# The first shift and scale of a two-layer backbone: from three engines to TensorE, inside the first projection's loop

## The chip, the core and the metric

One core of a Trainium2 chip runs the whole program in one launch. The metric is the device time of one execution in microseconds (us). The kernel before took 1386.01 us, the median of 3 runs (1384.87 to 1386.74).

## The reference, cut to what matters

Two layers work on 256 latent tokens `x` and 256 context tokens `ctx`, each 1024 wide. Each layer starts with a normalisation whose result is scaled and shifted by vectors that come from a conditioning vector; the first projection follows.

```python
silu_c = jax.nn.silu(c)
silu_cc = jax.nn.silu(c_ctx)
...
mx = (silu_c @ w_ada[l] + b_ada[l]).reshape(b, N_MOD, 1, D_MODEL)
mc = (silu_cc @ w_ada[l] + b_ada[l]).reshape(N_MOD, 1, 1, D_MODEL)
hx_n = _modulate(_rms_norm(h, norm1_g[l]), mx[:, 0], mx[:, 1])
hc_n = _modulate(_rms_norm(hc, norm1_g[l]), mc[0], mc[1])
...
ux = _split_cols(hx @ w_in)
uc = _split_cols(hc @ w_in)
```

`_modulate(h, shift, scale)` is `h * (1 + scale) + shift`. Shift and scale of layer 0 are two products of a vector of 1024 with a matrix of 1024 x 1024, for each of the two vectors `c` and `c_ctx`: the first two of the six parts of `w_ada[0]`. Behind the two layers stands a last normalisation.

## The kernel before, in words

Activations lie with the 1024 channels in eight blocks of 128 partitions and the 512 tokens (256 of the context, 256 latent) in the free dimension. The normalised and modulated input is kept as a pair `hn[k]` of a high part `hh` and a low part `hl`, in a reduced fp32 format, and so are the weights: a chunk of 128 x 1024 is loaded to `raw` (L99), ScalarE (ACT) casts it to the high part of `hl` (L117), VectorE (DVE) makes the low part (L107). A product is then three matmuls: high by high, high by low, low by high (`mm3`, L189 to L191). The program is recorded in the order in which it is written, engine by engine; there is no scheduler.

`start()` (from L417) does the head of layer 0. It loads `h`, sums the squares over the channels (L470 to L476), sums over the partitions with four matmuls (L269), takes the root with Newton steps on DVE (L257 to L259) and spreads the result `R` over the partitions (L283). silu of `c_ctx` and `c` is spread to all partitions as `cb[0]` and `cb[1]`.

Shift and scale of block k need the rows of two tiles of 128 x 1024 (`wa`, the transposed `w_ada`) multiplied with `cb` and summed. For `c` DVE does both in one instruction (L441); for `c_ctx` GpSimd (POOL) multiplies (L452) and ACT sums (L459). Two operations of 128x2 on DVE make the coefficients of it, `Ag` (L520) and `mods` (L522). `mod(k)` multiplies `h[k]` with `R` (L512, DVE), scales and shifts (L514, ACT, `v`), casts to `hh` (L516, ACT); L542 makes the low part on DVE.

The loop over the eight input blocks k then multiplies block k with eight weight blocks and adds to eight output banks at once, which are all of PSUM: `outs` is four `pg`, two `ps`, one `pt`, one `po`. In turn k the queues hold the coefficients of k+1 behind the work of k, so the small operations of DVE stand behind L441's long ones and wait for ACT's sums, and these for POOL's products.

```python
for i in range(8):
    mm3(outs[i], blk(k, i), hn[k], k == 0, k == KT - 1)
```

Behind the loop `mixer` takes the banks away: the first four go to `nakd` (ACT, L625) and `nakl` (DVE, L628), the others to `naq` (L635, L638). POOL clears `nakl` and `up` (L612, L614) and copies `nakd` (L629). `tokmajor` (L225) needs the four `pg` banks at once for the next 96 matmuls, with the weight chunks 8 to 11. The tiles of `start()` lie in a pool of their own (`sp`) which the mixer's tiles (`nakl`, `naq`, `up`) reuse.

Of the kernel before, what the change touches and what calls it, by code (L numbers as in the profile page):

```python
# [8 lines left out]
F32 = mybir.dt.float32  # L9
# [9 lines left out]
KT = 8  # L19
# [13 lines left out]
def hybrid_dit_kernel(ctx: ExitStack, tc: tile.TileContext, hT, wst, adaf, crow_d, vec_d,  # L33
# [69 lines left out]

    def prep_lo(i=total):
        while late and late[0][0] <= i:
            _, r, t = late.pop(0)
            V.tensor_tensor(t[:, 1], r, t[:, 0].bitcast(F32), op=ALU.subtract)  # L107

    def prep_to(i, wait=False):
        if not wait:  # L110
            prep_lo(i)
        while st["prep"] <= min(i, total - 1):
# [4 lines left out]
            S.copy(t[:, 0], r)  # L117
# [299 lines left out]
    def start():  # L417
        with tc.tile_pool(name="st", bufs=1) as sp:
            crow = sp.tile([1, 2048], F32, name="crow")
            nc.sync.dma_start(out=crow, in_=crow_d)  # L420
# [4 lines left out]
            make_identity(nc, ident)  # L425
            S.activation(tiny(1, "dummy"), eps, AF.Silu)

            acc = new_acc()
            gb = sp.tile([128, 8], F32, name="gb")
            V.scalar_tensor_tensor(gb, vec[:, V_BA + 8:V_BA + 16], 1.0, vec[:, V_N1:V_N1 + 8],  # L430
                                   op0=ALU.add, op1=ALU.mult)
            wa = {}
# [6 lines left out]
            def ada_v(k, ms=(0, 1)):  # L439
                for m in ms:  # L440
                    V.tensor_tensor_reduce(out=tmp().bitcast(BF16), in0=wa[k, m], in1=cb[1], scale=1.0,  # L441
                                           scalar=0.0, op0=ALU.mult, op1=ALU.add,
                                           accum_out=mods[0][:, m * 8 + k, 1:2])

            pr = {}

            def ada_p(k, ms=(1, 0)):
                if k >= KT:
                    return
                for m in ms:  # L450
                    t = pr[k, m] = sp.tile([128, 1024], F32, name="pr", tag="pr", bufs=4)
                    P.tensor_tensor(t, wa[k, m], cb[0], op=ALU.mult)  # L452

            def ada_s(k, ms=(1, 0)):
                if k >= KT:
                    return
                for m in ms:
                    t = pr[k, m]
                    S.activation(t, t, AF.Copy, accum_out=mods[0][:, m * 8 + k, 0:1])  # L459
# [889 lines left out]
```

## Time and profile before

| what | value |
|---|---|
| median of 3 runs | 1386.01 us (1384.87 to 1386.74) |
| the profiled execution: its time, its span | 1382.58 us, 1380.8 us |
| TensorE (PE) busy | 1322.7 us, 96% of the span |
| weight loads of PE (PEld) busy | 1147.2 us |
| DVE busy | 894.2 us |
| ACT busy | 597.2 us |
| POOL busy | 200.2 us |
| mean granted clock of PE | 0.987 |

Every trace time below counts from the start of the span of that one profiled execution, whose own time is 1.8 us longer than its span and 3.4 us below the median of the runs. A busy share is a mean over the whole span; what a stretch waits for is read from that stretch. In the rows, a line of the timeline gives the start, the length in which instructions of one kind follow each other, the engine, the source line, the operation, what it writes and reads, its shape and the count; at its end may stand the engine's idle time before it and what ended that.

### The profile page before, as it was taken

The page shows a single profiled execution, that of the slowest core. Times are in us where ns is not written, and L with a number is a line of the kernel's source. Part 1 is how long each engine was busy: PE and PEld are TensorE (multiplying, and loading weights), DVE is VectorE, ACT ScalarE, POOL GpSimd, SP SyncE. Part 2 cuts the span into 40 slices and gives each one's busy share as a digit, 9 for nine tenths or more (in the row PEclk, how much of TensorE's full clock was granted, in tenths as well). Part 3 has the DMA queues.
Part 4 walks back from the last instruction along what each step waited for, and adds up shares of the span by engine and source line. Part 5 has one row for each costly group of instructions (what it writes and reads, how often), then busy time and mean ns, then how long its engine had stood idle before and what let it go on. Part 6 is the DMA issues. An engine that isn't in the chain of part 4 may idle for free.

```text
span 1380.8 us, 19738 instructions
## 1 busy us (share of the span) xinstructions
PE 1322.7 (96%) x7658; PEld 1147.2 (83%) x7658; DVE 894.2 (65%) x1467; ACT 597.2 (43%) x929; POOL 200.2 (14%) x230
## 2 busy tenths in 40 slices
PE   4799999899999999999999999999999989999997
PEld 2578777688888888888888888988889989899997
DVE  8997554766877766565555653665538877655555
ACT  5484554544232435232123232465556545544453
POOL 6652302412000001000000000142134200000000
PEclk9999999999999999999999999999999999999999
DMA  7433322433545624355445653243435665455553
GB/s 261 168 110 117 98 71 83 128 123 122 183 162 162 201 71 138 124 171 165 155 139 172 211 183 99 70 140 108 142 122 185 217 237 177 151 184 195 183 171 106
DMA packets 62304, 207.27 MB, mean 150 GB/s; under 512 B 7041, under 2 KB 11521, under 8 KB 62209
## 3 DMA queue, kind: packets, MB, share of 16 engines
q1 hardware_dynamic: 50546, 163.97, 36.3%
q10 hardware_dynamic: 11664, 42.04, 9.2%
q8 instruction: 60, 0.98, 0.3%
q14 instruction: 34, 0.28, 0.1%
HBM read 204.94 MB, written 1.05 MB: 149 GB/s over the span
## 4 chain that ended last, share of the span: by engine, by line
PE 87%; DVE 8%; ACT 2%; issue 2%; DMA 0%; POOL 0%; SPq 0%; DVEq 0%; ACTq 0%; POOLq 0%
PE pg L189 26%; PE pg L190 26%; PE pg L191 26%; PE po L941 1%; DVE hl L107 1%; DVE tmp L441 1%; PE pt L675 1%; PE po L687 1%; DVE mods L522 1%; PE ps L643 1%; PE ps L644 1%; DVE rkl L876 0%; ACT hl L117 0%; DVE acc L476 0%; ACT hh L310 0%
## 5 line engine op out<-in xcount | busy, mean ns | idle before, releaser
L189 PE MATMUL pg<-hh,hl 128*128 128x256 f32 (+1 forms) x1568 | 530.9, 339 | 15.2 <-ACT hh L516 12.7
L191 PE MATMUL pg<-hl,hl 128*128 128x256 f32 (+1 forms) x1568 | 527.4, 336 | 2.2 <-DVE hl L542 1.6
L190 PE MATMUL pg<-hh,hl 128*128 128x256 f32 (+1 forms) x1568 | 526.2, 336 | 1.4 <-DVE hl L107 1.4
L107 DVE TENSOR_TENSOR hl<-raw,hl 128x1024 fp32r<-128x1024 f32 x276 | 342.3, 1244 | 174.8 <-ACT hl L117 169.8
L117 ACT CAST hl<-raw 128x1024 fp32r<-128x1024 f32 x276 | 287.6, 1046 | 207.5 <-PE pg L191 108.0
L189 PEld LDWEIGHTS pg<-hh,hl 128*128 128x128 f32 x1568 | 302.0, 193 | 48.7 <-ACT hh L516 15.1
L191 PEld LDWEIGHTS pg<-hl,hl 128*128 128x128 f32 x1568 | 301.7, 192 | 34.6 <-DVE hl L542 4.3
L190 PEld LDWEIGHTS pg<-hh,hl 128*128 128x128 f32 x1568 | 301.9, 193 | 32.1 <-DVE hl L107 2.1
L378 DVE CUSTOM_DVE_ANT_0 tmp<-ada,cb 128x1024 bf16<-128x1024 f32 x128 | 156.1, 1226 | 27.1 <-DMA ada<-in_adaf 17.8
L189 PE MATMUL pg<-fh,hl 128*128 128x256 f32 (+1 forms) x374 | 121.6, 325 | 0.0
L190 PE MATMUL pg<-fh,hl 128*128 128x256 f32 (+1 forms) x374 | 121.4, 325 | 0.0
L191 PE MATMUL pg<-fl,hl 128*128 128x256 f32 (+1 forms) x374 | 121.4, 325 | 0.0
L319 POOL TENSOR_TENSOR hl<-tmp,hh 128x256 fp32r<-128x256 f32 x20 | 14.8, 738 | 627.4 <-ACT hh L308 371.1
L291 ACT CAST fh<-sg 128x512 fp32r<-128x512 f32 (+1 forms) x44 | 22.6, 513 | 140.9 <-DVE sg L1150 140.9
L190 PEld LDWEIGHTS pg<-fh,hl 128*128 128x128 f32 x374 | 70.1, 188 | 7.2
L189 PEld LDWEIGHTS pg<-fh,hl 128*128 128x128 f32 x374 | 70.1, 187 | 7.1
L191 PEld LDWEIGHTS pg<-fl,hl 128*128 128x128 f32 x374 | 70.1, 187 | 7.1
L335 DVE SCALAR_TENSOR_TENSOR h<-pg,mods,h 128x256 f32<-128x256 f32 x72 | 32.7, 480 | 65.8 <-PE pg L191 65.7
L1150 DVE TENSOR_TENSOR sg<-pg,sg 128x512 f32<-128x512 f32 (+1 forms) x44 | 24.5, 557 | 51.1 <-PE pg L191 47.7
L1000 ACT ACTIVATE tmp<-pg 128x512 f32<-128x512 f32 (+1 forms) x48 | 23.5, 490 | 77.2 <-PE pg L191 76.2
L1147 ACT ACTIVATE sg<-pg 128x512 f32<-128x512 f32 (+1 forms) x44 | 21.6, 491 | 69.2 <-PE pg L191 69.2
L189 PE MATMUL pg<-hl,hh 128*128 128x512 f32 x128 | 50.6, 395 | 0.0
(241 smaller groups left out, 1643.4 us busy)
## 6 DMA issues: line engine op xcount, KB each, us to landing
raw<-in_wst SPq DMA_DIRECT2D x276, 512.0 KB, 3.6
ada<-in_adaf ACTq DMA_DIRECT2D x80, 512.0 KB, 3.8
wa<-in_adaf SPq DMA_DIRECT2D x16, 512.0 KB, 4.5
h<-in_hT SPq DMA_DIRECT2D x16, 256.0 KB, 5.0
bm<-in_bias SPq DMA_DIRECT2D x32, 128.0 KB, 2.0
out<-yt SPq DMA_DIRECT2D x4, 256.0 KB, 2.8
cs<-in_rope SPq DMA_DIRECT2D x2, 256.0 KB, 3.0
pw<-in_pw SPq DMA_DIRECT2D x2, 256.0 KB, 3.6
```

The lines of the kernel that those rows point to most:

```text
L107: V.tensor_tensor(t[:, 1], r, t[:, 0].bitcast(F32), op=ALU.subtract)
L117: S.copy(t[:, 0], r)
L189: TE.matmul(o, wh, xh, start=a, stop=False)
L190: TE.matmul(o, wl, xh, start=False, stop=False)
L191: TE.matmul(o, wh, xl, start=False, stop=z)
L291: S.copy(d0, src)
L319: P.tensor_tensor(hn[k][1][:, c], t[:, c], hi, op=ALU.subtract)
L335: V.scalar_tensor_tensor(h[k][:, c], o, mods[l][:, col + k, s:s + 1], h[k][:, c], op0=ALU.mult, op1=ALU.add)
L378: V.tensor_tensor_reduce(out=tmp().bitcast(BF16), in0=tiles[n], in1=cb[s], scale=1.0, scalar=0.0, op0=ALU.mult, op1=ALU.add, accum_out=mod ...
L1000: S.activation(sg[f][:, cl], o, AF.Sigmoid)
L1147: S.activation(e["s"][:, c], o, AF.Silu)
L1150: V.tensor_tensor(e["s"][:, c], o, e["s"][:, c], op=ALU.mult)
```

## The change

All of the first shift and scale is multiplied on PE. The weights come untransposed (`adan`, 1 MB per block k, one load instead of two of 512 KB). `csil` holds silu of the two vectors in two of 32 columns, the rest is zero. For block k, `nat_first` (new L459) multiplies eight pieces `csil[:, kb]` (128 x 32) with `wn[k][:, kb]` (128 x 256) in plain fp32; the pieces write four strips of 32 partitions of one bank, in turn, so each strip holds a part of the sum. `nat_copy` (L463) brings the bank to SBUF, and `nat_second` (L469) multiplies it with `sel`, which adds the four strips and turns the result by 90 degrees: two matmuls of two columns. The two small operations of DVE follow (L470, L472).

The bank that this needs is `outs[7]`. The loop therefore accumulates only seven output blocks; the weights of the eighth are kept (`w7`, high and low part) and its 24 matmuls follow behind the loop. The first eight weight chunks are cast in two pieces, 896 and 128 columns. `cb` is still needed later, and is now spread by 16 matmuls with the identity and copied by ACT. Two of the squares move from POOL to DVE.

```diff
+    def parts(j, t):
+        if j >= KT:
+            return [(t, slice(0, 1024))]
+        return [(t[:, :, :896], slice(0, 896)), (st["w7"][:, :, j], slice(896, 1024))]
...
-            S.copy(t[:, 0], r)
+            for a, b in parts(j, t):
+                S.copy(a[:, 0], r[:, b])
...
-            def ada_load(k):
-                for m in (1, 0):
-                    t = wa[k, m] = sp.tile([128, 1024], F32, name="wa", tag="wa", bufs=6)
-                    nc.sync.dma_start(out=t, in_=adaf[0, m * 8 + k])
...
+            def nat_load(k):
+                if k < KT:
+                    wn[k] = sp.tile([128, 8, 256], F32, name="wn", tag="wn", bufs=3)
+                    nc.sync.dma_start(out=wn[k], in_=adan[k])
...
+            outs = [pg() for _ in range(4)] + [pS(), pS(), pT(), pO()]
+            nat = outs[7]
+
+            def nat_first(k):
+                for kb in range(8):
+                    g = slice(32 * (kb % 4), 32 * (kb % 4) + 32)
+                    TE.matmul(nat[g, :256], csil[:, kb], wn[k][:, kb], start=(kb < 4), stop=(kb >= 4))
...
+            def nat_second(k, t):
+                o = nat[:, 256:260]
+                for i in range(2):
+                    TE.matmul(o[:, 2 * i:2 * i + 2], t[:, i * 128:(i + 1) * 128], sel, start=True, stop=True)
+                V.tensor_scalar(Ag[0][:, 0, k, :], o[:, 0:2], vcol(0, V_N1, k), gb[:, k:k + 1],
+                                op0=ALU.mult, op1=ALU.add)
+                V.tensor_scalar(mods[0][:, k, :], o[:, 2:4], vcol(0, V_BA, k), None, op0=ALU.add)
...
+            for k in range(KT):
+                nat_load(k + 3)
+                load_to(k + 3)
+                more = k + 1 < KT
+                if more:
+                    nat_first(k + 1)
                     prep_to(k + 1, True)
-                ada_p(k + 2)
-                if k + 1 < KT:
-                    ada_v(k + 1, (1,))
...
+                    t = mult(k + 1)
+                    tn = nat_copy()
+                block(k, 0)
+                block(k, 1)
+                if more:
+                    nat_second(k + 1, tn)
                     prep_lo()
...
-                for i in range(8):
-                    mm3(outs[i], blk(k, i), hn[k], k == 0, k == KT - 1)
+                    mod(k + 1, t)
+                for i in range(2, 7):
+                    block(k, i)
+            for k in range(KT):
+                mm3(outs[7], (w7[:, 0, k], w7[:, 1, k]), hn[k], k == 0, k == KT - 1)
```

On PE, at the end of turn 0 and the start of turn 1, there stood before the blocks of `pt` and `po` and at once the next input block (`hh1`):

```order
L191 MATMUL pt_233<-hl0_86,hl_224 128x512
L189 MATMUL po_234<-hh0_85,hl_224 128x512
L190 MATMUL po_234<-hh0_85,hl_224 128x512
L191 MATMUL po_234<-hl0_86,hl_224 128x512
L189 MATMUL pg_227<-hh1_87,hl_251 128x512
L190 MATMUL pg_227<-hh1_87,hl_251 128x512
L191 MATMUL pg_227<-hl1_88,hl_251 128x512
```

The same place now (`mm3` has become L196 to L198):

```order
L198 MATMUL pt_157<-hl0_86,hl_235 128x512
L459 MATMUL po_158<-wn_147,csil_129 32x256 x8
L196 MATMUL pg_151<-hh1_87,hl_265 128x512
L197 MATMUL pg_151<-hh1_87,hl_265 128x512
L198 MATMUL pg_151<-hl1_88,hl_265 128x512
L196 MATMUL pg_152<-hh1_87,hl_265 128x512
L197 MATMUL pg_152<-hh1_87,hl_265 128x512
L198 MATMUL pg_152<-hl1_88,hl_265 128x512
L469 MATMUL po_158<-sel_135,wt_321 128x2 x2
L196 MATMUL pg_153<-hh1_87,hl_265 128x512
```

The eighth block is gone from the turn; the product group of the block after next stands in its place, and two small matmuls stand behind the first two blocks.

On DVE one turn held before, with two long operations of L441, each followed by the reading of its sum, among the others:

```order
L520 TENSOR_SCALAR Ag_81<-mods_79,vec,gb 128x2
L522 TENSOR_SCALAR mods_79<-mods_79,vec 128x2
L512 TENSOR_TENSOR tmp<-h_113,Rs 128x512
L441 ISA tmp,mods_79<-wa,cb_78 128x1024
L441 ISA mods_79 128x1
L107 TENSOR_TENSOR hl<-raw,hl 128x1024
L542 TENSOR_TENSOR hl_94<-v,hh_93 128x512
L441 ISA tmp,mods_79<-wa,cb_78 128x1024
```

One turn of DVE now:

```order
L510 TENSOR_TENSOR tmp<-h_111,Rs 128x512
L463 COPY wt<-po 128x256
L470 TENSOR_SCALAR Ag_81<-po,vec,gb 128x2
L472 TENSOR_SCALAR mods_79<-po,vec 128x2
L113 TENSOR_TENSOR hl<-raw,hl 128x896
L113 TENSOR_TENSOR w_138<-raw,w_138 128x128
L519 TENSOR_TENSOR hl_94<-v,hh_93 128x512
```

The multiply with `Rs` now stands ahead of the coefficients, the long operations of L441 are gone, and a copy and a second piece of the weights' low part have come.

On DVE behind the loop, where the first banks are taken away, the waits (named in brackets, by the engine or DMA queue whose count is waited for) were:

```order
L394 TENSOR_TENSOR lga<-lga,vec 128x8 [waits DVE_49]
L628 TENSOR_TENSOR nakl_656<-pg,nakd_664 64x512 [waits PE_49,Activation_49,Pool_49]
L628 TENSOR_TENSOR nakl_657<-pg,nakd_665 64x512
L628 TENSOR_TENSOR nakl_658<-pg,nakd_666 64x512 [waits PE_49,Activation_49]
L628 TENSOR_TENSOR nakl_659<-pg,nakd_667 64x512
```

and are now:

```order
L401 TENSOR_TENSOR lga<-lga,vec 128x8 [waits DVE_49]
L628 TENSOR_TENSOR nakl_685<-pg,nakd_693 64x512 [waits DMAHW3_49,DMAHW5_49,PE_49,DMAHW7_49,Activation_49,Pool_49]
L628 TENSOR_TENSOR nakl_686<-pg,nakd_694 64x512
L628 TENSOR_TENSOR nakl_687<-pg,nakd_695 64x512 [waits Activation_49]
L628 TENSOR_TENSOR nakl_688<-pg,nakd_696 64x512
```

The order of the operations is the same. The count of PE that the first of them waits for was that of the last matmul of the first bank; in the built program it is now that of the last of the 24 matmuls behind the loop, since `nakl` lies where `w7` lay. POOL's first clearing operation (L610) waits for the same count.

## Rows read from the trace of the kernel before

**Rows 1.** The page: engine's busy time (share) xinstructions; a costliest group, busy, mean ns.

```profile
PE 1322.7 (96%) x7658; PEld 1147.2 (83%) x7658; DVE 894.2 (65%) x1467; ACT 597.2 (43%) x929; POOL 200.2 (14%) x230
...
L107 DVE TENSOR_TENSOR hl<-raw,hl 128x1024 fp32r<-128x1024 f32 x276 | 342.3, 1244 | 174.8 <-ACT hl L117 169.8
```

**Rows 2.** Windows: stretch, length, busy PE, PEld, DVE, ACT, POOL; PEclk, DMA share, GB/s.

```profile
10.00:20.00 10.00, 1.95 (x9) 1.78 (x8) 9.65 (x9) 5.87 (x10) 8.71 (x3) 1.00 1.02 413
30.00:79.00 49.00, 37.86 (x122) 27.11 (x122) 49.00 (x50) 26.81 (x46) 27.96 (x10) 0.90 0.45 150
79.00:95.00 16.00, 15.96 (x70) 13.25 (x71) 13.50 (x25) 14.29 (x24) 5.94 (x13) 1.00 0.51 171
```

**Rows 3.** Waits from 30 to 79 us: total us, times, longest.

```profile
PE pg L189 <- ACT hh L516: 12.7, 6, 3.8
```

**Rows 4.** Timeline: POOL's products, DVE's small operations beside and without them.

```profile
11.29 16.75 POOL L452 TENSOR_TENSOR pr<-wa,cb 128x1024 f32<-128x1024 f32 x6 [1.59 <-ACT sq L470]
...
20.14 2.26 DVE L258 SCALAR_TENSOR_TENSOR nt<-nt,ms 128x4 f32<-128x4 f32 x1
...
42.13 5.63 POOL L452 TENSOR_TENSOR pr<-wa,cb 128x1024 f32<-128x1024 f32 x2 [3.58 <-ACT pr L459]
...
43.11 2.34 DVE L520 TENSOR_SCALAR Ag<-mods,vec,gb 128x2 f32<-128x2 f32 x1
...
85.00 0.28 DVE L520 TENSOR_SCALAR Ag<-mods,vec,gb 128x2 f32<-128x2 f32 x1
...
86.11 1.10 ACT L514 ACTIVATE v<-tmp,mods,Ag 128x256 f32<-128x256 f32 x2 [0.17 <-DVE tmp L512]
...
87.89 0.69 DVE L542 TENSOR_TENSOR hl<-v,hh 128x512 fp32r<-128x512 f32 x1 [0.69 <-ACT hh L516]
```

**Rows 5.** Timeline of PE: the first blocks, the last two turns, the first matmul behind.

```profile
30.68 0.79 PE L189 MATMUL pg<-hh,hl 128*128 128x512 f32 x1 [3.78 <-ACT hh L516]
...
36.15 0.45 PE L189 MATMUL ps<-hh,hl 128*128 128x512 f32 x1
...
84.16 0.39 PE L189 MATMUL pg<-hh,hl 128*128 128x512 f32 x1
...
95.04 0.39 PE L189 MATMUL pg<-hl,hh 128*128 128x512 f32 x1
```

**Rows 6.** Timeline of the start (DVE, PE), and of a later normalisation at the full clock.

```profile
8.79 5.79 DVE L476 TENSOR_TENSOR acc<-acc,sq 128x512 f32<-128x512 f32 x4 [0.31 <-ACT sq L470]
...
14.64 1.87 PE L269 MATMUL ps<-ones,acc 128*128 128x1 f32 x8 [4.56 <-DVE acc L476]
24.85 2.05 PE L283 MATMUL pt<-ident,rstd 128*128 128x128 f32 x8 [8.34 <-DVE rstd L259]
...
506.94 0.50 PE L269 MATMUL ps<-ones,acc 128*128 128x1 f32 x4
...
508.82 0.60 PE L283 MATMUL pt<-ident,rstd 128*128 128x128 f32 x4
```

**Rows 7.** Timeline of PE: fp32 matmuls on strips of 64, neighbours, and 512 columns.

```profile
2.92 7.16 PE L481 MATMUL pg<-crow,ones 1*128 1x512 f32 x8 [2.92 <-DMA crow<-in_crow]
...
146.34 0.39 PE L191 MATMUL pg<-hl,hl 128*128 128x512 f32 x1
146.65 1.95 PE L687 MATMUL po<-pt,nav 128*64 128x256 f32 x16
148.53 0.66 PE L675 MATMUL pt<-ident,p 128*128 128x128 f32 x4
```

**Rows 8.** Timeline behind the loop: POOL and DVE.

```profile
89.34 4.44 POOL L612 MEMSET nakl<- 64x512 f32 x8
...
92.63 5.66 DVE L628 TENSOR_TENSOR nakl<-pg,nakd 64x512 fp32r<-64x512 f32 x8 [1.42 <-ACT nakd L625]
...
95.83 6.21 POOL L629 CAST nakd<-nakd 64x512 fp32r<-64x512 f32 x8
...
110.02 3.49 DVE L107 TENSOR_TENSOR hl<-raw,hl 128x1024 fp32r<-128x1024 f32 x3
```

More of the change, by code (lines that the diff above doesn't have):

```diff
@@ L116, in prep_to @@
             r = raw_t.pop(j)
-            S.copy(t[:, 0], r)
+            for a, b in parts(j, t):
+                S.copy(a[:, 0], r[:, b])
             late.append((j, r, t))
@@ L425, in start @@
             make_identity(nc, ident)
+            csil = sp.tile([128, 8, 32], F32, name="csil")
+            P.memset(csil, 0.0)
             S.activation(tiny(1, "dummy"), eps, AF.Silu)
@@ L439, in ada_v @@
[L439 to L452, printed above, removed]
@@ new lines, in start, with nat_copy @@
+            for k in range(3):
+                nat_load(k)
+                load_to(k)
+            outs = [pg() for _ in range(4)] + [pS(), pS(), pT(), pO()]
[4 more added lines that the diff above has]
+                    TE.matmul(nat[g, :256], csil[:, kb], wn[k][:, kb], start=(kb < 4), stop=(kb >= 4))
+            def nat_copy():
+                t = sp.tile([128, 256], F32, name="wt", tag="wt", bufs=2)
+                V.tensor_copy(t, nat[:, :256])
+                return t
@@ L468, in sq_k, with spread @@
+            sqrt_table()
+            for i in range(4):
+                for b in range(4):
+                    kb = 4 * (i % 2) + b
+                    TE.matmul(outs[i][:, b * 128:(b + 1) * 128], csil[:, kb, i // 2:i // 2 + 1].to_broadcast([128, 128]),
+                              ident, start=True, stop=True)
+            def spread(i):
+                S.copy(cb[i // 2][:, (i % 2) * 512:(i % 2) * 512 + 512], outs[i])
+            for k in range(KT):
                 t = sp.tile([128, 512], F32, name="sq", tag="sq", bufs=4)
-                if eng is S:
+                if k in (2, 5):
+                    V.tensor_tensor(t, h[k], h[k], op=ALU.mult)
+                else:
@@ L470, in sq_k @@
                     S.activation(t, h[k], AF.Square)
-                else:
-                    eng.tensor_tensor(t, h[k], h[k], op=ALU.mult)
                 if k == 0:
@@ L476, in sq_k, with mult, mod @@
                     V.tensor_tensor(acc, acc, t, op=ALU.add)
[L478 removed]
+                if k in (3, 4, 6):
+                    spread(max(k - 3, 0) - (k > 4))
+            o = outs[4]
             for i in range(4):
[L480 to L502 removed]
+                TE.matmul(o[:, i:i + 1], acc[:, i * 128:(i + 1) * 128], ones[:, 0:1], start=True, stop=True)
             y = norm_rstd(o, 4)
[L504 to L506 removed]
+            spread(3)
+            R = norm_bcast(y, range(4), outs[6])
+            nat_first(0)
+            t0 = nat_copy()
             prep_to(0, True)
             Rs = sp.tile([128, 512], F32, name="Rs")
[L510 to L511 removed]
+            def mult(k):
+                t = tmp()
                 V.tensor_tensor(t, h[k], R if k == 0 else Rs, op=ALU.mult)
+                return t
+            def mod(k, t):
+                v = sp.tile([128, 512], F32, name="v", tag="sq", bufs=4)
                 for s, c in enumerate((CTX, X)):
```

87 lines of the change are left out of this document (19 added, 68 removed).

## The prediction

> **What bounds the kernel now.** The page is read first. TensorE (PE) is busy 96% of the span [rows 1], so in most of the program nothing else shortens the time. The question is where PE isn't full, and the 10 to 95 us stretches of the windows view answer it [rows 2]: from 10 to 20 us PE works 1.95 of 10 us, from 30 to 79 us 37.86 of 49 us while VectorE (DVE) works all 49, and from 79 us on PE is full (15.96 of 16). The granted clock of 0.90 in the middle row says that part of the time ran at the lower level, 1.2 GHz. The waits of that stretch name the cause: PE stood 12.7 us for the shifted and scaled block `hh` of L516 [rows 3], and the two 128x2 coefficients before it come late on DVE. The timeline shows why DVE is late [rows 4]. In one turn L520, an operation of two columns, takes 2.34 us beside a POOL product (L452, 42.13 to 47.76 us); the same operation takes 0.28 us at 85.00, when POOL has stopped. At the start it is the same: L258, four columns, takes 2.26 us beside POOL's 16.75 us of products. So the head of the kernel, up to about 79 us, is bound by DVE, and largely by DVE being held while POOL multiplies. The reader should see that PE could do the 64 blocks in 64 x 0.68 = 43.5 us (below), and needs from 30.68 to 95.04.
>
> All sums below are for one number: when PE begins the work after the eight output blocks, 95.04 us now [rows 5]. From there PE is full, so I carry a shift of that moment to the end of the program unchanged.
>
> **The price of the old matmuls.** From 84.16 to 95.04 there are 48 starts, 0.227 us apart [rows 5]; a block of three costs 0.68, a turn of seven blocks 4.76, the last 24 matmuls 5.44. The first twelve at the low clock, with the wait for the first low part, took 30.68 to 36.15, 5.47 instead of 2.72: 2.75 us more.
>
> **The change, part by part.**
>
> *POOL's products, DVE's reduces and ScalarE's (ACT's) sums go.* These are what held the coefficients. All small DVE operations then cost what they cost at 85 us. A turn of DVE has left one multiply and one low part (0.69 each [rows 4]), a copy of 256 columns (at most 0.69), two small operations (0.28 each) and the low part of the weights (1.24 [rows 1], now in two pieces, perhaps 0.1 more): about 4.0 us, below PE's turn, so DVE stops being the bound. ACT has a weight cast, 1.10 for `v` and a cast, some 3 us; splitting its cast is hidden there.
>
> *The start.* The last four additions of the squares begin at 8.79 and take 5.79 us beside POOL [rows 6]; at the 0.7 of a 512-column operation they end at 11.6 instead of 14.58. The two squares that move from POOL to DVE fit its waits for `h` before that. Then, all at the low clock as before: four column sums 1.87, the root and three Newton steps 1.38 (from the end of L269 at 507.44 to L283 at 508.82, free of POOL), the broadcast 2.05 [rows 6]: 16.9. The first product group, 2.0 (below): 18.9; a copy and two small matmuls (half of 1.87) with their handovers: 20.4; two coefficients 0.5: 20.9; `v` to `hh`, 86.11 to 87.9 [rows 4]: **22.7** for the first block instead of 30.68. The 16 matmuls that spread silu(c) lie before 11.6: 32 records like L283's eight in 2.05 are 8.2 us, from about 3.5. The new 1 MB loads carry the bytes of the two halves they replace; at 413 GB/s [rows 2] the 3.1 MB of the first two pairs of loads need 8 us after `h`, which ends them before they are used.
>
> *The product groups.* Eight fp32 matmuls per turn, 256 columns, each on 32 of PE's 128 columns, four strips in turn. No such operation is in the trace; the nearest is L687: 16 records (two for each of eight fp32 matmuls), same 256 columns, strips of 64 in pairs. The matmul before it starts at 146.34, the one after the group at 148.53 [rows 7]: less 0.23 for the former, 1.96 us. Records in a row would take 16 x 0.227 = 3.6, since an fp32 record passes its columns twice: L481's eight records of 512 columns take 7.16 us, 0.9 each, where the first twelve of [rows 5] are 0.46 apart. So pairs run side by side: 8 rounds of 0.215 and 0.24 of entry and exit. If four strips run side by side as two do, 4 x 0.215 + 0.24 = **1.1 us**. Bounds: 0.9 without entry and exit, 3.9 with no overlap at all. I take 1.1, the pattern of the nearest row extended to four. At the low clock that is 2.0.
>
> The Trainium skill's "TensorE: Matmul & The Clock Gate", section "Measured speedup vs the span model", speaks against a full factor of four: four row strips gave 3.07 times, three column strips 2.38. By it the group would be an estimated 3.6 / 3.07 + 0.24 = 1.4 us, and the total about 3 us later; no run here shows four strips.
>
> *The second matmuls.* Two per turn, two columns each, four records: L269 at the full clock has four in 0.50 [rows 6]. Their input copy lies beside blocks 0 and 1 (1.36 us), so I charge no wait.
>
> *The chain inside a turn.* After the second matmuls the next block's chain runs beside blocks 2 to 6 and the next product group, 3.4 + 1.1 = 4.5 us. It costs 85.00 to 87.9 without the multiply, which now comes earlier, some 2.5 to 3.1 us for `hh`; the low part is wanted 0.45 later than `hh`. Slack is over 1 us, so I charge 0.1 a turn. The prepared weights come before the low part on DVE and fit the same slack.
>
> *The eighth block.* It moves 24 matmuls to the end; nothing is added to PE. But the kept weights lie in memory that the mixer's `nakl` tiles reuse: in the new program L628's first eviction waits for the very last of these matmuls, where it began at 92.63, before PE was through [rows 8]. The first bank is free after two of its eight operations (5.66 / 8 each): 0.2 + 1.42 = 1.6 us in which PE has no bank for `tokmajor`. Queued behind them on DVE are the evictions of `naq`, the decay logarithms and the low part of chunk 11 (first of three at 110.02 [rows 8], done 18.5 us after L628 began). PE wants it 16.8 us after `tokmajor` begins. So the true price is 0.2 + 18.5 - 16.8 = **1.95 us**. ACT's casts of `nakd`, on the contrary, get 7 us of cover. POOL's clearing of `nakl` and what follows it up to its copies (89.34 to 95.83), and the copies (6.21) [rows 8], had begun beside the last blocks; now they begin after them and end some 13 us later. The first scores that read them stand behind most of `tokmajor`'s 96 matmuls of 0.227, 21.8 us, so I charge nothing; with that cover gone it would be rival 4.
>
> **Sum.** 22.7 + 2.75 (low clock, first low part) + 56 x 0.68 = 38.1 + 6 x 1.1 (the first two groups lie in the start) = 6.6 + 7 x 0.5 = 3.5 + 0.7 + 5.44 = 79.8; with the eviction 1.95: **81.75 instead of 95.04, 13.3 us less**. The profiled execution, 1382.58 us, would become 1369.3. It lies 3.4 below the median of the runs shown, 1386.01; against that the time is **1372.7 us**.
>
> **Rivals.**
> 1. *The four strips run only two at a time*: 1.96 a group. Six groups add 5.2; the two of the start, at the low clock, 2.7. 7.9 in all, a gain of 5.4: 1380.6. For it: each fp32 matmul is two records that use the same strip, and two side by side is all the trace shows. Against: the pairs of L687 begin 0.215 apart, as long as one record, so it's the columns that limit and not the issue.
> 2. *The strips don't overlap*: 3.9 a group at full clock, 6.9 at the low one. Six add 16.8, the first two 4.9 and 4.3 (part of the latter lies beside the start's chain), so 26 against 13.3: about 12.7 slower, 1398.7. This is the case of the other sign; it decides from about 2.5 us a group. For it: all eight write one bank. Against: L687's pairs write one bank as well.
> 3. *The chain is the bound*, a turn being limited by nat_copy, the coefficients, `v`, `hh` and the low part in a ring with little slack. Each us beyond the slack costs 7. I price 1 us: 1379.7. For it: six handovers between engines; against: 85.00 to 88.58 [rows 4] holds all but one of them.
> 4. *The eviction costs more*, since POOL's clearing (7 us) and DVE run at once after the blocks and DVE was seen to be held by POOL: up to 4 us more, 1376.7. Against: POOL's clearing and copies ran beside L628 before, too, at 0.7 an operation [rows 8].
>
> **How the numbers follow.** Forecast 0.55 (its own range 1368 to 1376.5), rival 1 0.17, rival 2 0.07, rival 3 0.12, rival 4 0.09. The low end takes a start 2 us earlier, groups of 0.9 and no low clock: 1366.5. The high end takes rivals 1 and 3: 1382. A measurement of this kernel can tell about 0.2%, 2.8 us, from no change. Forecast, rivals 1 (mostly), 3 and 4 are faster by more: 0.88. Same 0.05 (rival 1 with a worse eviction), slower 0.07 (rival 2).
>
> **What would show it.** Right: product groups of about 1.1 us, the first block at about 22 to 23 us, turns of 6.5 us with PE full from then on, no POOL product, small DVE operations below 0.3, a PE gap of about 2 us before or in `tokmajor` with L628 as releaser. Wrong: groups of 2 or 4 us (rivals 1, 2); idle time of PE before L196 each turn with ACT `hh` or before L469 with DVE as releaser (rival 3); a gap over 4 us after the blocks (rival 4); a later stretch that has become longer than before, which would break the step that carries the shift to the end.

## The result and the profile after

The changed kernel takes **1367.41 us** (median of 4 runs, 1365.9 to 1368.76), the kernel before, beside it, 1385.67 us (4 runs, 1384.87 to 1386.74). The ratio is 0.9865, 95% interval 0.9852 to 0.9877: 1.2 to 1.5% faster. The profiled execution of the changed kernel took 1367.57 us with a span of 1365.8 us, 15.0 us less than that of before [rows 1]; the medians are 18.3 us apart. That these two differ is the point on which the prediction's number was off, and the last experiments are about it. The ratios below leave out one run of 1669 us, at a granted clock of 0.75, of the ten runs of the kernel with one strip.

The page's first part, for the engines (busy time, share of the span, instructions):

```profile
PE 1326.2 (97%) x7842; PEld 1151.9 (84%) x7842; DVE 847.6 (62%) x1454; ACT 580.7 (43%) x907; POOL 152.7 (11%) x213
```

PE has 3.5 us more to do than in [rows 1] and the program is shorter all the same: time went where PE stood still. Both stretches of [rows 2] that held that idle time, in the windows view (columns as in [rows 2]):

```profile
10.00:20.00 10.00, 5.59 (x34) 4.54 (x36) 4.10 (x10) 2.82 (x6) 0.00 (x0) 0.63 1.00 414
30.00:79.00 49.00, 49.00 (x292) 36.69 (x291) 23.15 (x49) 25.17 (x43) 0.00 (x0) 1.00 0.53 177
```

From 30 to 79 us PE now works all 49 us where it worked 37.86, at the full clock instead of 0.90, and DVE works 23.15 us where it worked all 49. What PE still waits for between 12 and 110 us, beside two waits of 0.5 us at the start (total us, times, longest):

```profile
PE ps L499 <- DVE acc L494: 3.2, 1, 3.2
PE pg L196 <- DVE nakl L628: 1.7, 1, 1.7
PE pt L290 <- DVE rstd L266: 1.2, 1, 1.2
```

The 12.7 us of [rows 3], PE's wait for `hh` in six of eight turns, are gone; within a turn PE waits for nothing. One new wait has come, the second line. PE's timeline shows the places that the sum of the prediction speaks of, the first block, one product group and its second matmuls, and the first matmul behind the blocks:

```profile
13.77 1.86 PE L499 MATMUL ps<-ones,acc 128*128 128x1 f32 x8 [3.19 <-DVE acc L494]
18.86 1.94 PE L459 MATMUL po<-wn,csil 128*32 128x256 f32 x16
24.71 0.80 PE L196 MATMUL pg<-hh,hl 128*128 128x512 f32 x1
...
63.05 0.39 PE L198 MATMUL pt<-hl,hl 128*128 128x512 f32 x1
63.37 1.07 PE L459 MATMUL po<-wn,csil 128*32 128x256 f32 x16
64.37 0.50 PE L196 MATMUL pg<-hh,hl 128*128 128x512 f32 x1
65.88 0.50 PE L469 MATMUL po<-sel,wt 128*128 128x2 f32 x4
66.24 0.48 PE L196 MATMUL pg<-hh,hl 128*128 128x512 f32 x1
...
81.86 0.47 PE L196 MATMUL pg<-hl,hh 128*128 128x512 f32 x1 [1.73 <-DVE nakl L628]
```

The work behind the blocks begins at 81.86 us instead of 95.04 [rows 5]. From 81.86 to the end are 1283.9 us, where before there were 1285.8: the remaining 1.8 of the 15.0 us.

DVE in one of the turns, the copy and the first of the two coefficients:

```profile
64.50 0.42 DVE L463 COPY wt<-po 128x256 f32<-128x256 f32 x1 [1.07 <-PE po L459]
66.42 0.28 DVE L470 TENSOR_SCALAR Ag<-po,vec,gb 128x2 f32<-128x2 f32 x1 [1.49 <-PE po L469]
```

The operation of two columns that took 2.34 us beside POOL's product [rows 4] takes 0.28, and DVE now waits for PE, not PE for DVE.

### The profile page after: what moved, and what is told of

The parts are those of the page before. It is cut to its first block, busy times and chain, and to the rows that moved or that the text cites. A ratio compares the mean times of both kernels' runs of the same rounds, so it can differ in the third digit from the quotient of the medians.

```text
span 1365.8 us, 20012 instructions
## 1 busy us (share of the span) xinstructions
PE 1326.2 (97%) x7842; PEld 1151.9 (84%) x7842; DVE 847.6 (62%) x1454; ACT 580.7 (43%) x907; POOL 152.7 (11%) x213
## 3 DMA queue, kind: packets, MB, share of 16 engines
HBM read 204.93 MB, written 1.05 MB: 151 GB/s over the span
## 4 chain that ended last, share of the span: by engine, by line
PE 89%; DVE 6%; ACT 3%; issue 1%; DMA 1%; POOL 0%; DVEq 0%; ACTq 0%; SPq 0%; POOLq 0%
PE pg L196 26%; PE pg L197 26%; PE pg L198 26%; PE po L941 1%; PE po L687 1%; PE pt L675 1%; DVE hl L113 1%; PE po L459 1%; PE ps L643 1%; PE ps L644 1%; DVE nakl L628 1%; DMA bm<-in_bias 1%; DVE rkl L876 0%; DVE naq L638 0%; DVE acc L494 0%
## 5 line engine op out<-in xcount | busy, mean ns | idle before, releaser
L196 PE MATMUL pg<-hh,hl 128*128 128x256 f32 (+1 forms) x1568 | 528.1, 337 | 2.5 <-ACT tmp L1000 1.4
L198 PE MATMUL pg<-hl,hl 128*128 128x256 f32 (+1 forms) x1568 | 523.3, 334 | 0.6 <-POOL hl L326 0.5
L113 DVE TENSOR_TENSOR hl<-raw,hl 128x1024 fp32r<-128x1024 f32 (+1 forms) x276 | 341.4, 1241 | 172.2 <-ACT hl L124 166.9
L124 ACT CAST hl<-raw 128x1024 fp32r<-128x1024 f32 (+1 forms) x276 | 286.9, 1043 | 211.4 <-PE pg L198 112.3
L196 PEld LDWEIGHTS pg<-hh,hl 128*128 128x128 f32 x1568 | 299.7, 191 | 36.1 <-issue 3.8
L198 PEld LDWEIGHTS pg<-hl,hl 128*128 128x128 f32 x1568 | 299.2, 191 | 30.6 <-POOL hl L326 1.4
L196 PE MATMUL pg<-fh,hl 128*128 128x256 f32 (+1 forms) x374 | 121.6, 325 | 0.0
L198 PE MATMUL pg<-fl,hl 128*128 128x256 f32 (+1 forms) x374 | 121.4, 325 | 0.0
L196 PEld LDWEIGHTS pg<-fh,hl 128*128 128x128 f32 x374 | 70.1, 187 | 7.2
L198 PEld LDWEIGHTS pg<-fl,hl 128*128 128x128 f32 x374 | 70.1, 187 | 7.2
L196 PE MATMUL pg<-hl,hh 128*128 128x512 f32 x128 | 50.8, 397 | 1.7 <-DVE nakl L628 1.7
```

Source lines behind the costliest of these rows:

```text
L113: V.tensor_tensor(a[:, 1], r[:, b], a[:, 0].bitcast(F32), op=ALU.subtract)
L124: S.copy(a[:, 0], r[:, b])
L196: TE.matmul(o, wh, xh, start=a, stop=False)
L198: TE.matmul(o, wh, xl, start=False, stop=z)
```

## Experiments

Three questions were open. Was it POOL's products that held DVE, or the amount of DVE's work? What do the added parts cost (strips, the wait behind the blocks, the first group in the start's chain)? And why did the runs fall by more than the profiles?

### What held DVE

**POOL's products taken out of the kernel before.** ACT now sums the rows as they are, so this kernel leaves out the multiplication with silu of `c_ctx`; all else stays.

```diff
-                    P.tensor_tensor(t, wa[k, m], cb[0], op=ALU.mult)
...
-                    S.activation(t, t, AF.Copy, accum_out=mods[0][:, m * 8 + k, 0:1])
+                    S.activation(t, wa[k, m], AF.Copy, accum_out=mods[0][:, m * 8 + k, 0:1])
```

> The kernel before without POOL's products: ACT sums the rows of wa as they are, so the multiplication with silu(c_ctx) is left out, and everything else (DVE's long L441 operations, all 192 matmuls in eight banks, the small operations on SBUF) stays. Theory (DVE was held by POOL's products, not full of its own work): DVE's two-column operations fall from 2.3 to 0.3 us, the first block starts at 22 to 25 us, a turn takes 5.5 to 6.2 us, 16 to 24 us faster than the kernel before. Rival (the long operations and reduces on DVE and ACT's sums bound the turn by themselves): a turn stays above 7 us, less than 8 us faster.

Measured: 1355.79 us against 1386.79 for the kernel before on the same chip, ratio 0.9777 (0.9761 to 0.9793), 31.0 us less. The first block, the start of a later turn and the first matmul behind the blocks in PE's timeline:

```profile
22.34 0.80 PE L189 MATMUL pg<-hh,hl 128*128 128x512 f32 x1 [2.62 <-ACT hh L515]
...
36.36 0.39 PE L189 MATMUL pg<-hh,hl 128*128 128x512 f32 x1
41.80 0.39 PE L189 MATMUL pg<-hh,hl 128*128 128x512 f32 x1
...
69.00 0.39 PE L189 MATMUL pg<-hl,hh 128*128 128x512 f32 x1
```

A turn is 5.44 us, which is PE's own time for its 24 matmuls, although DVE keeps both of its long operations. So the theory holds, and more strongly than I put it: with POOL quiet, neither DVE nor ACT bounds a turn at all.

The edit also spares ACT its wait for the product, but that wait did not set DVE's pace: DVE worked all 49 us of [rows 2]. The rows of DVE show where its time went, first before, behind the L520 of 43.11 us in [rows 4], then without the products:

```profile
45.37 2.42 DVE L522 TENSOR_SCALAR mods<-mods,vec 128x2 f32<-128x2 f32 x1
52.33 2.36 DVE L520 TENSOR_SCALAR Ag<-mods,vec,gb 128x2 f32<-128x2 f32 x1
```
```profile
30.60 0.29 DVE L519 TENSOR_SCALAR Ag<-mods,vec,gb 128x2 f32<-128x2 f32 x1
35.56 0.29 DVE L519 TENSOR_SCALAR Ag<-mods,vec,gb 128x2 f32<-128x2 f32 x1
```

Before, DVE went round once in 9.22 us (from 43.11 to 52.33), of which the two operations of two columns took 4.59 (from 43.11 to the next operation at 47.70). Without the products it goes round in 4.96, and the two take 0.33. The 4.26 us that they lose are the whole difference.

The run also shows what the changed kernel pays for its way of freeing DVE. In the changed kernel the work behind the blocks begins 12.86 us later than in this run. A turn of the changed kernel takes 6.50 us, of which 4.76 are the seven blocks; the other 1.74, six times, are 10.4. The first block is 2.37 later, the new wait 1.89, one pair of small matmuls in turn 0 0.36; against that, matmuls at the lower rate cost 1.0 in the first turn instead of 3.1 here. Together 12.9. (The lower rate is read here from the spacing of the matmuls, 0.43 us instead of 0.227; the column of the granted clock says 1.00 in the start of this run and of before.)

**All four long operations of a turn on DVE**, none on POOL, ACT or PE, so that nothing is left out:

```diff
+                    for s in (0, 1):
-                    V.tensor_tensor_reduce(out=tmp().bitcast(BF16), in0=wa[k, m], in1=cb[1], scale=1.0,
+                        V.tensor_tensor_reduce(out=tmp().bitcast(BF16), in0=wa[k, m], in1=cb[s], scale=1.0,
...
-                ada_p(k + 2)
-                if k + 1 < KT:
-                    ada_v(k + 1, (1,))
...
-                ada_s(k + 1)
                 if k + 1 < KT:
-                    ada_v(k + 1, (0,))
+                    ada_v(k + 1)
```

> The kernel before with all four long multiply-and-sum operations of a turn on DVE, where POOL multiplied and ACT summed two of them; no product on POOL or PE, nothing left out. Theory (a product of POOL costs DVE more than the same work on DVE itself): a turn of DVE is 4 x 1.15 + 1.14 + 0.6 + 0.6 + 0.35 = 7.3 us where it was 9.2, the first block comes at 23 to 25 us, and PE starts the work behind the blocks at 24 + 7 x 7.3 + 5.44 = 80 to 82 us, as the changed kernel does: 12 to 17 us faster than the kernel before. Rival (DVE is full anyway, so that more work on it makes the turn longer): turns above 9.2 us, slower than before.

Measured: 1373.61 us against 1385.56, ratio 0.9919 (0.9902 to 0.9935), 12.0 us less; the work behind the blocks begins at 86.55. DVE's timeline shows a turn (the second `hl` row ends it):

```profile
39.62 0.69 DVE L537 TENSOR_TENSOR hl<-v,hh 128x512 fp32r<-128x512 f32 x1 [0.68 <-ACT hh L514]
40.23 1.22 DVE L442 CUSTOM_DVE_ANT_0 tmp<-wa,cb 128x1024 bf16<-128x1024 f32 x1
...
47.75 0.69 DVE L537 TENSOR_TENSOR hl<-v,hh 128x512 fp32r<-128x512 f32 x1 [0.67 <-ACT hh L514]
```

The direction is the theory's: DVE does twice its old share of the long operations and the kernel is faster than with POOL's help. The size was missed: 12.0 us is the lower end of the 12 to 17, and the work behind the blocks begins 4.5 us after the 82 that I put as the latest. A turn is 8.13 us, not 7.3, mostly since DVE waits 0.67 us for `hh` in each.

**POOL's products put back into the changed kernel**, two per turn, with a result that nobody uses:

```diff
+            pd = [sp.tile([128, 1024], F32, name="pd", tag="pd", bufs=2) for _ in range(2)]
...
+                for i in range(2):
+                    P.tensor_tensor(pd[i], cb[0], cb[1], op=ALU.mult)
```

> The changed kernel with two products of POOL of 128 x 1024 per turn added that nobody uses. Theory (POOL's products hold the small operations of DVE, 2.3 us instead of 0.28, whatever they read): the coefficients of a turn come 3 to 5 us later than before, over the slack of 1 us, so 10 to 25 us slower than the changed kernel, with PE waiting for hh. Rival (only operations that read and write SBUF are held, those that read PSUM are not, or the chain has slack enough): within 2 us.

Measured: 1399.55 us, 32.1 above the changed kernel, ratio to before 1.0095 (1.008 to 1.011). It isn't the slow chain of turns that I expected. Nothing paces these products, so POOL runs all sixteen in a row, and nearly the whole loss is one stall of DVE, for which PE waits 26.97 us:

```profile
16.06 37.11 POOL L537 TENSOR_TENSOR pd<-cb,cb 128x1024 f32<-128x1024 f32 x16 [14.32 <-ACT cb L483]
```
```profile
16.21 2.28 DVE L266 SCALAR_TENSOR_TENSOR rstd<-nt,sq 128x4 f32<-128x4 f32 x1
22.55 0.42 DVE L463 COPY wt<-po 128x256 f32<-128x256 f32 x1 [4.06 <-PE po L459]
22.89 0.68 DVE L510 TENSOR_TENSOR tmp<-h,pt 128x512 f32<-128x512 f32 x1
24.08 0.28 DVE L470 TENSOR_SCALAR Ag<-po,vec,gb 128x2 f32<-128x2 f32 x1 [0.51 <-PE po L469]
24.28 0.21 DVE L472 TENSOR_SCALAR mods<-po,vec 128x2 f32<-128x2 f32 x1
24.40 29.72 DVE L113 TENSOR_TENSOR hl<-raw,hl 128x896 fp32r<-128x896 f32 x1
```
```profile
54.18 0.80 PE L197 MATMUL pg<-hh,hl 128*128 128x512 f32 x1 [26.97 <-DVE hl L113]
```

The work behind the blocks begins at 114.11 us, 32.25 later than in the changed kernel: 26.97 in this wait, 1.70 in a later first block, and most of the rest in matmuls at the lower clock (0.50 granted from 54 to 60 us).

Both theories have a share. All these operations of DVE ran beside POOL. L266 and L113, which read only SBUF, were held: the first for one product (2.28 instead of 0.16 us), the second until the last of POOL's products was through, 29.72 us where it takes 1.08. The four that read PSUM (`po`, `pt`) took their usual 0.42, 0.68, 0.28 and 0.21. So, as far as these rows go, the coefficients of the changed kernel would not be held by POOL any more, as those of before were, since they now come from PSUM; the low part of the weights still would. Why L113 was let in at none of the gaps between products, and L266 at the first, stays open. The Trainium skill, "SBUF — State Buffer", section "SBUF: two separate sides", says that a GpSimd operation that reads SBUF and a DVE operation with two inputs in SBUF share a pair of ports, which whichever starts first has to itself for its whole instruction. The rows agree on who is held and who isn't; that an operation stands for 29.72 us, over some twelve instructions of POOL (2.35 us each), is more than that sentence says.

### What the added parts cost

**Two strips instead of four, and one instead of four**, all else as in the changed kernel (the copy and the second matmuls take 64 and 32 partitions):

```diff
-                    g = slice(32 * (kb % 4), 32 * (kb % 4) + 32)
-                    TE.matmul(nat[g, :256], csil[:, kb], wn[k][:, kb], start=(kb < 4), stop=(kb >= 4))
+                    g = slice(32 * (kb % 2), 32 * (kb % 2) + 32)
+                    TE.matmul(nat[g, :256], csil[:, kb], wn[k][:, kb], start=(kb < 2), stop=(kb >= 6))
```
```diff
-                    g = slice(32 * (kb % 4), 32 * (kb % 4) + 32)
-                    TE.matmul(nat[g, :256], csil[:, kb], wn[k][:, kb], start=(kb < 4), stop=(kb >= 4))
+                    TE.matmul(nat[0:32, :256], csil[:, kb], wn[k][:, kb], start=(kb == 0), stop=(kb == 7))
```

> The eight product matmuls of a group take two strips of 32 columns in turn, the rest of the change stays. Theory (a pair of strips runs side by side as L687's pair of 64 does, time goes with the number of rounds): a group of 8 rounds x 0.227 + 0.24 = 2.0 us instead of 1.09, six groups add 5.5 us, the two at the start up to 3: 6 to 9 us slower than the changed kernel. Rival (the limit is the issue of records, not the strips): within 1 us.

> All eight product matmuls of a group accumulate on one strip of 32 columns; the sum is the same. Theory (the four strips run side by side and PE is full in the loop): a group at full clock takes 16 x 0.227 + 0.24 = 3.9 us instead of 1.09, so six groups add 16.5 us and the two at the start, at the low clock, 4 to 5 us each, partly hidden: 20 to 26 us slower than the changed kernel. Rival (the sixteen records were not what bounded the turn, or strips did not run side by side): within 2 us.

Measured: two strips 1376.25 us, 8.8 more than the changed kernel (ratio to before 0.9928, 0.9914 to 0.9943); one strip 1389.74 us, 22.3 more (1.0024, 1.0015 to 1.0034). PE's timeline with two strips, then with one:

```profile
61.23 1.92 PE L459 MATMUL po<-wn,csil 128*32 128x256 f32 x16
63.08 0.50 PE L196 MATMUL pg<-hh,hl 128*128 128x512 f32 x1
```
```profile
62.09 3.64 PE L458 MATMUL po<-wn,csil 128*32 128x256 f32 x16
65.66 0.50 PE L196 MATMUL pg<-hh,hl 128*128 128x512 f32 x1
```

From the group's start to the next matmul it is 3.57 us on one strip, 1.85 on two, 1.00 on four: the sixteen records are the same, and time goes with the number of rounds. This settles the prediction's largest unknown: four strips gain a factor of 3.57 over one. The Trainium skill's "TensorE: Matmul & The Clock Gate", section "Measured speedup vs the span model", has no row for four column strips; the 3.07 of its four row strips, by which the prediction made its estimate, was too low for them here, and the measurement decides. These two kernels stand for rivals 1 and 2 of the prediction: 1376 and 1390 us, where it put 1380.6 and 1398.7.

**The wait behind the blocks.** The chapter on the change said that `nakl` lies where `w7` lay. It doesn't: in the built program the first `nakl` tile lies over the product weights `wn` and touches no address of `w7`. The wait on the last of the 24 matmuls comes from another side: the start's pool `sp` is given back as a whole, and the tiles that follow wait for the last reader of any tile in it. Before, PE's last reading of that pool was the spreading of `crow` at the start; now it is the eighth block's reading of `w7`. So `w7` was moved to another pool:

```diff
-            st["w7"] = w7 = sp.tile([128, 2, 8, 128], F32R, name="w7")
+            st["w7"] = w7 = [wp.tile([128, 8, 128], F32R, name="w7", tag="ada", bufs=2) for _ in range(2)]
...
```

> The kept weights of the eighth block are two tiles in the pool of the later weight chunks instead of the start's own pool, so the first evictions behind the loop wait only for the last matmul of their own bank. Theory (the gap of PE before the work behind the blocks is the wait on the release of the start's pool): the 1.9 us gap before L196 with L628 as releaser goes, 1.5 to 2.3 us faster than the changed kernel. Rival (DVE is late anyway, from its own work or POOL's clearing): the gap stays, within 0.5 us.

The last matmul of the eighth block and the first behind it, and the first eviction on DVE:

```profile
78.72 0.39 PE L199 MATMUL po<-hl,w 128*128 128x512 f32 x1
78.94 0.39 PE L197 MATMUL pg<-hl,hh 128*128 128x512 f32 x1
```
```profile
73.53 5.66 DVE L629 TENSOR_TENSOR nakl<-pg,nakd 64x512 fp32r<-64x512 f32 x8 [1.41 <-ACT nakd L626]
```

The gap is gone: 0.22 us between the two matmuls, and the eviction starts 5.2 us before the last matmul of the eighth block does. So the cause of the gap is shown. In the runs the gain doesn't show: 1367.1 us (1366.1 to 1367.6; ratio to before 0.9863, 0.9846 to 0.9879), 0.3 under the changed kernel, where 1.5 to 2.3 were expected. Four runs of the changed kernel, or of these variants of it, lie 1.5 to 4 us apart, so 1.9 us can't be told this way; the combination below tells more.

**The first product group out of the start's chain.**

```diff
+            nat_first(0)
+            t0 = nat_copy()
             o = outs[4]
...
             y = norm_rstd(o, 4)
+            nat_second(0, t0)
             spread(3)
...
-            nat_first(0)
-            t0 = nat_copy()
...
-            nat_second(0, t0)
```

> The first product group and its copy stand ahead of the column sums of the squares, its two small matmuls ahead of the broadcast, its coefficients behind the Newton steps; everything else is the changed kernel. Theory (the group of 1.94 us, its copy and the two small matmuls lie on the path that sets the first block): the weights land at 13.3 us, the group ends at 15.2, the sums at 17.1, and the first block starts at 22.8 instead of 24.7; 1.9 us less at the work behind the blocks. Since each low-clock stretch further on comes in steps that cost 1.7 us, the time falls by 0 to 4 us. Rival (the first block waits for something else, as ACT's casts or the loads): it starts within 0.4 us of 24.7.

> The early first group and the kept weights outside the start's pool, together. Theory: the two gains are in different places and add, 1.9 at the first block and 2.9 at the work behind the blocks (of which 1.9 is the gap), so that work starts at 76.5 to 78.5 us instead of 81.86; how much of the 3.4 to 5 us reaches the end depends on the low-clock stretches further on: 1362 to 1367 us. Rival (what is won in the head is given back in full at later waits): 1367 us or more.

> The early first group and the kept weights apart, once more, for its difference to the changed kernel on the same chip. Theory (the gains of the two edits in the head reach the end up to steps of 1.7 us): 1.5 to 4.5 us less than the changed kernel. Rival (the first difference of 2.8 us came from the chips): within 1 us of it.

Alone, with the early group, the first block comes at 23.28 us, later than the 22.8 worked out, and the work behind the blocks at 79.98, 1.88 earlier. That this is the edit isn't shown: a second profile of the unchanged kernel, in the next part, has 23.03 and 79.70. The runs give 1367.61 us, ratio to before 0.9862 (0.9848 to 0.9877), no difference from the changed kernel that these runs can tell. With both edits 1364.61 us (0.9838, 0.9823 to 0.9853), and once more 1363.08 us (0.9836, 0.9822 to 0.9851), beside 1368.72 for the changed kernel on that chip (0.9877, 0.9862 to 0.9892). The second profile with both:

```profile
20.23 0.50 PE L197 MATMUL pg<-hh,hl 128*128 128x512 f32 x1 [0.75 <-ACT hh L520]
...
75.04 0.39 PE L197 MATMUL pg<-hl,hh 128*128 128x512 f32 x1
```

With both edits the first block comes at 20.71 and 20.23 us in the two profiles, where the changed kernel had 24.71 and 23.03: that difference is larger than the one between two profiles of one kernel. The work behind the blocks begins at 77.41 us in the first profile with both, where 76.5 to 78.5 were expected, and at 75.04 in the second. The difference of 5.6 us on one chip is above the 4.5 that I put as the upper end; the 2.8 before it came from runs that did not stand side by side. Together the edits gain some 3 to 6 us, and this is the fastest version tried that leaves nothing out.

### Why the runs fell by more than the profiles

> The kernel before, unchanged, profiled once more. Theory (the profiled execution of before, 1382.58 us, lay 3.4 us under its median because its later low-clock stretches were short by one or two steps of 1.7 us): this one takes 1384 to 1388 us, and the difference to the first profile stands in one or two places, at 240 to 290 us or 1020 to 1190 us, and not in the head, where PE starts the work behind the blocks at 95.0 again. Rival (the head varies): that moment differs by more than 1 us.

> The kernel before, unchanged, a third profile. Theory (the head of before varies with the moment at which the loads release POOL's first product, and its first profile was an early one): PE starts the work behind the blocks at 96 to 100 us, the column sums of the squares at 15 to 19 us, and both move together. Rival (the second profile was the exception): 94.5 to 95.5 us again.

> The changed kernel, unchanged, beside the version with both edits and on the same chip. Theory (its head does not vary as that of before does, since no POOL product runs there): PE starts the work behind the blocks at 81.4 to 82.4 us again, 1366 to 1369 us. Rival (the head varies by several us as in before): that moment moves by more than 1 us.

These are the two kernels, unchanged. The column sums of the squares, the first block and the first matmul behind the blocks in the second profile of before, and under them the same three in the third:

```profile
18.13 1.87 PE L269 MATMUL ps<-ones,acc 128*128 128x1 f32 x8 [8.18 <-DVE acc L476]
33.00 0.80 PE L189 MATMUL pg<-hh,hl 128*128 128x512 f32 x1 [2.62 <-ACT hh L516]
99.05 0.39 PE L189 MATMUL pg<-hl,hh 128*128 128x512 f32 x1
```
```profile
15.72 1.87 PE L269 MATMUL ps<-ones,acc 128*128 128x1 f32 x8 [5.98 <-DVE acc L476]
31.75 0.79 PE L189 MATMUL pg<-hh,hl 128*128 128x512 f32 x1 [3.78 <-ACT hh L516]
97.77 0.39 PE L189 MATMUL pg<-hl,hh 128*128 128x512 f32 x1
```

With 1385.64 and 1384.25 us these executions lie where before's runs do, and they differ from the first profile, whose 1382.58 us lie below every run of before on record (the lowest is 1383.42), in the head: 99.05 and 97.77 us where the first had 95.04 [rows 5]. My theory for the second profile, that the head would stand at 95.0 again and later low-clock stretches would differ, fell; its rival held. The third lies in the ranges put down for it, but not by the cause named there: POOL's first product began at 11.29, 11.93 and 12.47 us in the three, which isn't the order of their heads. The first block comes later, at 33.00 and 31.75 us instead of 30.68, behind DVE's additions of the squares. In the second profile six of them stand beside POOL's products:

```profile
8.85 9.23 DVE L476 TENSOR_TENSOR acc<-acc,sq 128x512 f32<-128x512 f32 x6 [0.93 <-POOL sq L472]
```
```profile
11.93 16.23 POOL L452 TENSOR_TENSOR pr<-wa,cb 128x1024 f32<-128x1024 f32 x6 [1.49 <-DMA wa<-in_adaf]
```

Six additions take 9.23 us here; the four that were left from 8.79 us on in the first profile took 5.79 [rows 6]. In the third profile the last four took 5.66, no longer than in the first, and only began later, at 10.00. What lies ahead of both is the landing of `h`: POOL's first square, on which an addition waits, began at 5.79 us in the first profile and at 7.29 and 6.78 in the others. So the later landing is in both, more of the additions beside POOL in the second alone. The rest of the difference, 1.69 and 1.66 us between the first block and the work behind the blocks, stands beside the clock. The granted clock of the last stretch of [rows 2], 1.00 there, is lower in the second profile, and 0.89 in the third too:

```profile
79.00:95.00 16.00, 14.32 (x55) 11.33 (x56) 13.56 (x25) 13.74 (x23) 3.64 (x8) 0.89 0.50 167
```

The loop of both has one stretch at the lower level, 1.2 GHz, more than that of the first (four, not three). Its matmuls stand 0.43 us apart instead of 0.23, and some eight of them lie in it: about 1.6 us, by my estimate.

The head of the changed kernel varies as well, so my expectation of 81.4 to 82.4 us fell: its second profile has the work behind the blocks at 79.70. The first block came at 23.03 instead of 24.71. What differs is the granted clock of the start, the third number from the end; first profile, then second:

```profile
14.00:18.00 4.00, 2.78 (x13) 2.69 (x14) 0.73 (x5) 1.77 (x4) 0.00 (x0) 0.50 1.02 426
18.00:22.00 4.00, 3.46 (x25) 1.89 (x23) 1.02 (x2) 0.00 (x0) 0.00 (x0) 0.50 0.62 231
```
```profile
14.00:18.00 4.00, 2.78 (x15) 2.48 (x15) 0.73 (x5) 1.77 (x4) 0.00 (x0) 0.70 1.02 426
18.00:22.00 4.00, 2.94 (x37) 1.52 (x36) 2.29 (x5) 0.77 (x2) 0.00 (x0) 0.88 0.84 293
```

With the same work done by PE, the second had the column sums at the full clock (1.05 us instead of 1.86), the first group in part (1.52 instead of 1.94) and the second group whole (1.07 instead of 1.93).

Before that PE had done the same in both: its first 32 matmuls, to 10.58 and 10.35 us, and then a wait of 3.19 and 3.38 us for the squares. Why the clock fell sooner in the first (0.82 of full speed from 10 to 14 us, 1.00 in the second) isn't shown.

So the size of the gain comes out like this. Three profiles of before have their head at 95.04, 99.05 and 97.77, mean 97.3; two of the changed kernel at 81.86 and 79.70, mean 80.8: 16.5 us. From there to the end of the span before takes 1285.8, 1284.9 and 1284.7 us, the changed kernel 1283.9 and 1285.1: 0.6 less. Together 17.1, beside 18.3 in the first comparison of the runs and 16.8 in the second.

## Why the prediction was right, and where it was off

**What bounds the kernel: right.** POOL's products held DVE, DVE held the coefficients, these held PE. The run without the products shows it by itself: with POOL quiet a turn falls to PE's own 5.44 us, and the 4.26 us that DVE gains in each round are those of the two small operations.

**The start: two errors that cancel.** The first block was put at 22.7 us and came at 24.71, since the additions of the squares ended at 13.7 and not at 11.6 (ACT's last square waited for `h` until 10.72, and two squares stand among DVE's additions). The penalty of 2.75 us for the low clock behind it was mostly not paid: the first three matmuls took 1.45 us instead of 0.68 and the next ran at full clock. Together 25.5 us were predicted for both; it was 25.5. That is luck: in the second profile of the same kernel the first block came at 23.03.

**The product groups: right.** 1.1 us was taken, the pattern of L687 extended to four strips; it is 1.09 (from 63.28, where the matmul before it ends at 0.23 us, to 64.37). The two at the start took 1.94 and 1.93 at the low clock, 2.0 was said. The upper bound of 3.9 was near the mark too: the run on one strip has 3.57 from start to start, 3.66 measured as the 1.09 is.

**The second matmuls and the turn: right.** 0.36 instead of 0.5 a pair, but the matmuls after a group and after a pair come up to 0.1 later; a turn of 6.46 was worked out and 6.50 is there. PE never waits in a turn, so rival 3 has no part in it.

**The eighth block: the price right, the reason not.** 1.95 was worked out (its terms give 1.9), 1.6 of it at the first bank and the rest at chunk 11. 1.89 was measured at the first bank (79.97 to 81.86), since L628 began 0.35 us after the blocks and not 0.2, and 0.2 at chunk 11. That POOL's clearing runs beside it cost nothing, so rival 4 is out. That the wait comes from an overlap of addresses was wrong; it comes from the release of the whole pool.

**The sum up to the work behind the blocks**: 81.75 predicted, 81.86 measured in the first profile, 79.70 in the second. The terms of the loop are right; that the whole agrees to 0.1 us is luck of the start.

**From there to the time: the step that was off.** "The profiled execution, 1382.58 us, would become 1369.3. It lies 3.4 below the median of the runs shown, 1386.01; against that the time is 1372.7 us." The first sentence came within 1.8 us: 1367.57. The second added before's offset to the changed kernel, as if it were a constant of the measurement. It was a property of that one execution: a head of 95.04 where two others had 97.8 and 99.1. The column sums of the squares, whose last additions stand beside POOL's products there, began at 14.64, 18.13 and 15.72 us in the three; in the two profiles of the changed kernel at 13.77 and 13.73. That fits a start which varies because of the collision, but isn't proof of it, since the loads of the start differ too. The changed kernel's profile lay 0.2 us above its median. So the forecast stood 5.3 us above the median of the runs; 1367.41 lies under the forecast's own range (1368 to 1376.5) and 0.9 above the low end of the full one. (The high end, 1382, doesn't follow from its terms: 7.9 of rival 1 and 7.0 of rival 3 on 1372.7 are 1387.6.) And "I carry a shift of that moment to the end of the program unchanged" was good to 1.8 us only: the program behind the head takes 1283.9 to 1285.8 us in five profiles. It is longer the more time PE spent at the lower clock between 200 and 1300 us: 13.7 us of it in the changed kernel's first profile (1283.9), 17.1 in its second and in the two later ones of before (1284.7 to 1285.1), 20.5 in before's first (1285.8).

## What to carry to other kernels

Before work is spread over DVE and POOL, look at what DVE's small operations last beside POOL's long ones: here 2.34 us instead of 0.28, and the same work done by DVE alone was 12 us faster than with POOL's help. A single profile is a sample: its offset to the median of the runs belongs to that execution, and is not to be added to a forecast for another kernel. When a tile must live beyond its stage, look in which pool it lies, since the next stage waits for its last reader, wherever the addresses are.

## What the runs showed of the hardware that was not expected

- An SBUF-only operation of DVE of 128x896 stood 29.72 us, until the last of sixteen POOL products in a row was through, while four operations that read PSUM ran beside the same products at their usual 0.21 to 0.68 us.
- Eight fp32 matmuls of 32 columns on one, two and four strips of one bank took 3.57, 1.85 and 1.00 us: strips of the same bank run side by side almost without loss.
- The same program, doing the same work, had 0.50 and 0.70 of the full clock from 14 to 18 us in two executions, and its first block 1.7 us apart. An edit in this start that is worth less than that is not to be judged by one profile.
